# Moving one scratch tile to another ring, two gate additions to VectorE and two row scalings to ScalarE in a two-layer encoder

## The chip, the cores and the metric

The kernel runs on one core of one Trainium2 chip. A core has TensorE (matmul, with its weight load shown apart), VectorE, ScalarE, GpSimd and SyncE; the profile calls them PE and PEld, DVE, ACT, POOL and SP. They run their own instruction streams in order and wait for each other by semaphores. Operands lie in SBUF, matmul results in PSUM, inputs and outputs in device memory, and DMA engines move data between them. The metric is the device time of one execution in microseconds, as a median over several runs.

## The reference

Two layers on 512 tokens of width 1024, in float32. Layer 0 mixes tokens by neighbourhood attention on a grid, layer 1 by latent attention; then both add a gated embedding. A last norm follows.

```python
for i in range(DEPTH):
    xn = rmsnorm(x, norm_g[i])
    y = mixer_na(...) if i % 2 == 0 else mixer_mla(...)
    h = x + y
    gate = jax.nn.sigmoid(rmsnorm(h, ple_norm[i]) @ ple_w_gate[i])
    x = h + gate * (p[i] @ ple_w_proj[i])
return rmsnorm(x, final_norm)
```

where `rmsnorm(x, g)` is `x * rsqrt(mean(x * x) + 1e-6) * g`.

## The kernel before

The 512 tokens are four row tiles (0 to 3) of 128 partitions. [...] Precision comes from splitting every operand into a high and a low part, so that each product is three matmuls: high by high, low by high, high by low. `load_w` (lines 70 to 88) loads a weight tile as `wraw`, ScalarE makes the high part (line 83) and GpSimd the low part (line 84). Nearly all matmuls of projections are issued in the helper `mms` (line 107).

**Pools.** A tile comes from a pool; tiles of one tag share a ring of buffers and wait for the oldest to be free. `const`, `big`, `zp` and `wp` are opened first and stay: `big` holds transposed activations, `wp` the weights. `small` follows, for one-column tiles, with rings of eight for the tags `mx`, `sm`, `rc`, `ss`, `rs` and `mn` and one buffer for `warm`; each buffer takes 32 bytes of a partition. All pools opened later stand behind it: `pre` (start), `na` (heads of layer 0), `out0` and `out1` (output projection and gate of each layer), and `mla`, `mlac`, `mlah` (layer 1's heads). In `out0` and `out1` some of the weights lie in the stage's own pool instead of `wp`: those with `extra` in `load_w`, and in layer 1's gate those for which `own` in `prep` (line 577) is false.

**Heads.** In layer 1's dense heads the scores multiply `ke` or `ko` by `qe` or `qo`, `ex` holds the exponentials, four matmuls by `ident` transpose them (line 139), and line 841 multiplies them by the values. Projections of `cT` (line 730) stand between them.

**The last gate.** Layer 1's gate is `gate_seven`: a product of two matrices that are each cut in 2 x 2 blocks, made from seven block products instead of eight, in the order 1, 7, 2, 6, 5, 3, 4. Each product is two row tiles (i = 0, 1) of twelve matmuls at line 635, in two chunks of six; the weights of product p are prepared in two pieces by `prep(p)`, which loads, splits on ScalarE (line 587) and on GpSimd (line 589). The pieces of products 1 and 5 lie in `wp`, those of product 2 in `out1`, and product 3 has one of each. Products 2, 3, 5 and 4 each complete two pieces of the result, and `finish(t, n, ...)` is called for row tile t and column half n:

- ScalarE takes the sigmoid in PSUM (line 595);
- `pe`, the embedding, is loaded by DMA (line 600);
- VectorE multiplies (line 601), and the product is added to the row tile `r` (line 603), on VectorE if `last` is set and else on GpSimd;
- `after(t, n, ...)`, which is `done` of layer 1 (from line 1060 on), is kept in the list `behind` and traced when the next `finish` has traced its sigmoid.

`done` adds up the squares of the piece on ScalarE (line 1069, tile `sq`), or on VectorE for the very last quarter (line 1065), makes the mean `mn` on VectorE (line 1070), multiplies a tile's first half by the final norm's gain on GpSimd (line 1073), and once both halves of a row tile are there raises the mean to the power -1/2 on GpSimd (line 1079, `rs`), scales the half that came last by `rs` and gain on VectorE (line 1080), scales the first half by `rs` (on GpSimd, line 1082, for tiles 0 and 1; on ScalarE, line 1084, for tiles 2 and 3), and stores both.

The copies at line 647 take product 6 out of its bank, and product 5 adds onto it in that bank, so product 5 can start only behind the first of them.

**What sets the order.** The code is traced in program order with some edges (`issue_after`), and a scheduler orders each engine's stream from dependences and its own cost estimates; on the chip each engine then keeps that order. Tile numbers behind names, as in `r_6090`, are given by the build: `r_6090`, `r_6092`, `r_6094` and `r_6096` are row tiles 0 to 3.

Of the kernel before, what the change touches and what calls it, by code (L numbers as in the profile page):

```python
# [13 lines left out]
F32 = mybir.dt.float32  # L14
F32R = mybir.dt.float32r
AF = mybir.ActivationFunctionType
ALU = mybir.AluOpType
AX = mybir.AxisListType
PSUM = bass.MemoryType.PSUM
P = 128  # L20
S = 512
# [19 lines left out]
class Trunk:  # L41
# [527 lines left out]
    def gate_seven(self, pool, layer, rh, res, after):  # L569

        nc = self.nc
        pieces = 0
        turns = 3 + self.wxn // 2
        W, A, Bk, s1, s17, s6 = {}, {}, {}, {}, {}, {}

        def prep(p):
            nonlocal pieces
            W[p] = []
            src = self.quarter[layer][p] if p < 4 else self.sums[layer][p]
            for c in range(2):  # L580
                own = pieces % turns < 3
                pieces += 1
                raw = self.wp.tile([P, 1024], F32, name="wraw", tag="wraw", bufs=3)
                q, n = (self.wp, 3) if own else (pool, self.wxn)
                hi, lo = (q.tile([P, 1024], F32R, name=t, tag=t if own else "w4", bufs=n) for t in ("whi", "wlo"))
                nc.sync.dma_start(raw, src[c * P:(c + 1) * P])
                nc.scalar.activation(hi, raw, AF.Copy)  # L587
                for o in (slice(0, S), slice(S, 2 * S)):
                    nc.gpsimd.tensor_tensor(out=lo[:, o], in0=raw[:, o], in1=hi[:, o].bitcast(F32), op=ALU.subtract)  # L589
                W[p].append((hi, lo))  # L590

        behind = []

        def finish(t, n, x, o=0, wd=S, last=False):
            sg = nc.scalar.activation(x, x, AF.Sigmoid, scale=rh[t])
            while behind:
                with self.tc.issue_after(sg.ins):
                    behind.pop()()
            pe = pool.tile([P, S], F32, name="pe", tag="pe", bufs=4)[:, :wd]
            nc.sync.dma_start(pe, self.pe[layer][t][:, n * S + o:n * S + o + wd])  # L600
            nc.vector.tensor_tensor(out=x if last else pe, in0=pe, in1=x, op=ALU.mult)
            r = res[t][:, n * S + o:n * S + o + wd]
            (nc.vector if last else nc.gpsimd).tensor_tensor(out=r, in0=r, in1=x if last else pe, op=ALU.add)
            behind.append(lambda: after(t, n, o, wd))

        mm = self.last_out
        order = (1, 7, 2, 6, 5, 3, 4)
        for p in order[:4]:
            prep(p)
        warm = self.small.tile([P, 1], F32, name="warm", tag="warm", bufs=1)  # L610
        nc.scalar.activation(warm, rh[3], AF.Sigmoid)
        halves = ((0, 256), (256, 256)) if layer == 1 else ((0, S),)
        banks = {1: "mm", 7: "T", 6: "S"}
        home = {2: 1, 5: 6, 3: 6, 4: 7}
        C = {}
        sub = lambda out, x, y: nc.vector.tensor_tensor(out=out, in0=x, in1=y, op=ALU.subtract)
        for k, p in enumerate(order):
            if 0 < k < 4:
                prep(order[k + 3])
            if p == 7:  # L620
                self.mixed(5)
            if p == 6:
                self.mixed(3)
            x = self.X[p]
            for i in range(2):
                for o, wd in halves if i and p in (7, 4) else ((0, S),):
                    c = slice(o, o + wd)
                    if p in banks:
                        C[p, i, o] = self.psum("O" if o else banks[p])[:, :wd]
                    ps = C[home.get(p, p), i, o]  # L630
                    m = [(x[:, 2 * s + i, k * P:(k + 1) * P], W[p][k // 2][r][:, k % 2 * S + o:k % 2 * S + o + wd])
                         for c in range(2) for s, r in ((0, 0), (1, 0), (0, 1)) for k in (2 * c, 2 * c + 1)]
                    for j, (l, r) in enumerate(m):
                        with self.tc.issue_after(mm.ins):
                            mm = nc.tensor.matmul(ps, l, r, start=j == 0 and p in banks,  # L635
                                                  stop=j == 11 and p in (2, 3, 4), skip_group_check=True)
                    if p == 1:
                        s1[i] = self.temp("s1")
                        nc.scalar.activation(s1[i], ps, AF.Copy)
                    elif p == 7:  # L640
                        nc.vector.tensor_tensor(out=ps, in0=ps, in1=s1[i][:, c], op=ALU.add)
                        if o == 0:
                            s17[i] = self.temp("s17")
                        nc.scalar.activation(s17[i][:, c], ps, AF.Copy)
                    elif p == 6:
                        s6[i] = self.temp("s6")
                        nc.scalar.activation(s6[i], ps, AF.Copy)
                        for (a, b, o), t in C.items():
                            if (a, b) == (7, i):
                                sub(t, t, s6[i][:, o:o + t.shape[1]])  # L650
                    elif p == 5:
                        q = self.psum("mm" if i else "T")
                        sub(q, ps, s17[i])
                        sub(ps, ps, s1[i])
                        finish(2 + i, 1, q)
                    elif p == 2:
                        finish(i, 0, ps)
                    elif p == 3:
                        finish(i, 1, ps, last=layer == 1)
                    else:  # L660
                        finish(2 + i, 0, ps, o, wd, layer == 1)
        while behind:
            behind.pop()()

    def mla_c(self, pool, xT, cT, sets):
        nc, a = self.nc, self.a
# [273 lines left out]
    def run(self):  # L940
        tc, nc, a = self.tc, self.nc, self.a
# [6 lines left out]
        with tc.tile_pool(name="pre", bufs=4, reuse_waits="tile") as pool:  # L948
            ones = [nc.const_aps.tensor(1.0, (P, n), mybir.dt.bfloat16) for n in (P, S)]
            ps = self.psum("T")  # L950
# [26 lines left out]
            ss = pool.tile([P, NT], F32, name="ssq", bufs=1)  # L977
# [23 lines left out]
        with tc.tile_pool(name="na", bufs=2, reuse_waits="tile") as pool:  # L1001
            last = self.na_heads(pool, xT, zs, oT)

        x1T = []
        for layer in range(2):
            with tc.tile_pool(name=f"out{layer}", bufs=4, reuse_waits="tile") as pool:
                seven = layer in SEVEN
# [47 lines left out]
                else:  # L1055
                    mean = {}

                    def done(t, n, o, w):
                        c = slice(n * S + o, n * S + o + w)
                        r = res[t]  # L1060
                        sq = pool.tile([P, D], F32, name="sq", tag="xn", bufs=2 - seven)
                        mn = self.small.tile([P, 1], F32, name="mn", tag="mn")
                        first, final = t not in seen, o + w == S and t in seen
                        if o:
                            nc.vector.tensor_tensor_reduce(sq[:, :w], r[:, c], r[:, c], 1.0 / D, mean[t], op0=ALU.mult,
                                                           op1=ALU.add, accum_out=mn)
                        else:
                            ss = self.small.tile([P, 1], F32, name="ss", tag="ss")
                            nc.scalar.activation(sq[:, :w], r[:, c], AF.Square, accum_out=ss)
                            nc.vector.tensor_scalar(mn, ss, 1.0 / D, mean.get(t, EPS), op0=ALU.mult, op1=ALU.add)  # L1070
                        mean[t] = mn
                        if first:
                            nc.gpsimd.tensor_tensor(out=r[:, c], in0=r[:, c], in1=gn[:, c], op=ALU.mult)
                            seen.add(t)
                        if not final:
                            return
                        f, l = (slice(0, S), slice(S, D))[::1 if n else -1]
                        rs = self.small.tile([P, 1], F32, name="rs", tag="rs")
                        nc.gpsimd.tensor_tensor(out=rs, in0=mn, in1=self.half, op=ALU.pow)
                        nc.vector.scalar_tensor_tensor(r[:, l], r[:, l], rs, gn[:, l], op0=ALU.mult, op1=ALU.mult)  # L1080
                        if seven and n:
                            nc.gpsimd.tensor_tensor(out=r[:, f], in0=r[:, f], in1=rs.to_broadcast([P, S]), op=ALU.mult)
                        else:
                            nc.scalar.activation(r[:, f], r[:, f], AF.Copy, scale=rs)
                        nc.sync.dma_start(a["out"][t][:, l], r[:, l])
                        (nc.scalar if o else nc.sync).dma_start(a["out"][t][:, f], r[:, f])
                if seven:
# [115 lines left out]
```

## Time and profile before

| What | us |
|---|---|
| Median of 3 runs (lowest, highest) | 668.08 (667.8, 668.46) |
| The profiled execution | 668.41 |
| Its span, from the first to the last instruction | 666.3 |
| TensorE busy, of the span | 655.2 |
| GpSimd busy | 424.5 |
| ScalarE busy | 421.8 |
| VectorE busy | 372.0 |

The mean granted TensorE clock of the profiled execution is 0.995 of full speed. A row of the timeline gives the start and the length in us, the engine, the source line, the operation, the tiles written and read, and how many like instructions it merges; in square brackets stands the idle time before it and what ended that. A row of the chain of work gives start, length and what was being done; the chain is followed back from the last instruction, at each step to what released it. Rows of the groups give the busy time of all, then the mean of one in ns. A matmul's end is modelled in the profile, so the spacing of matmuls is read from their starts. The 9.2 us from 657.1 to the end hold 0.12 us of TensorE.

### The profile page before, as it was taken

Reading aid. Unit: us, or ns where it says so; the run is one execution under the profiler, and the core shown is the slowest. Engines: PE = TensorE matmul, PEld = TensorE weight load, DVE = VectorE, ACT = ScalarE, POOL = GpSimd, SP = SyncE. Lnnn points to the kernel's source line nnn. Section 1 sums busy time; section 2 is a strip of 40 time slices with the busy share of each in tenths; the row PEclk is TensorE's granted clock in tenths of the full one; section 3 lists DMA queues with packets and bytes.
Section 4 is the critical chain, followed back from the end, with each engine's and each line's share of the span. In section 5 each row is a group of like instructions: output and inputs, shape, how many; then the busy total and the mean of one; then the engine's idle time right before and its main releaser. Section 6 shows DMA issues by size and latency. Waiting matters only on the chain.

```text
span 666.3 us, 10037 instructions
## 1 busy us (share of the span) xinstructions
PE 655.2 (98%) x3443; PEld 555.2 (83%) x3443; DVE 372.0 (56%) x815; ACT 421.8 (63%) x838; POOL 424.5 (64%) x358
## 2 busy tenths in 40 slices
PE   9999999999999999999999999999999999999994
PEld 6888888988988888888899888888888888888873
DVE  6180365736645514443524613888888875144856
ACT  7671686857767742543444635887989887437944
POOL 0395466876575765853054526786959887748994
PEclk9999999999999999999999999999999999999998
DMA  9949422966142136534133335120111222664524
GB/s 323 343 149 329 159 89 90 206 154 162 58 146 76 64 141 253 190 103 139 79 111 108 106 94 154 53 76 18 54 49 63 65 89 103 229 244 160 166 93 150
DMA packets 37681, 90.62 MB, mean 136 GB/s; under 512 B 4416, under 2 KB 13376, under 8 KB 37568
## 3 DMA queue, kind: packets, MB, share of 16 engines
q1 hardware_dynamic: 33040, 85.02, 37.9%
q0 software_dynamic: 4160, 4.19, 4.0%
q10 hardware_dynamic: 432, 0.79, 0.3%
q8 instruction: 27, 0.44, 0.3%
q14 instruction: 22, 0.18, 0.1%
HBM read 78.45 MB, written 16.78 MB: 143 GB/s over the span
## 4 chain that ended last, share of the span: by engine, by line
PE 93%; POOL 2%; DMA 1%; issue 1%; DVE 1%; ACT 1%; POOLq 0%; DVEq 0%
PE ps_mm L107 42%; PE ps_S L107 13%; PE ps_mm L730 6%; PE ps_T L139 6%; PE ps_O L841 4%; PE ps_T L107 3%; PE ps_O L107 3%; PE ps_T L238 2%; PE ps_O L402 2%; PE ps_S L635 2%; PE ps_mm L184 2%; PE ps_T L390 2%; PE ps_mm L635 1%; PE ps_S L354 1%; PE ps_S L353 1%
## 5 line engine op out<-in xcount | busy, mean ns | idle before, releaser
L84 POOL TENSOR_TENSOR wwlo<-wraw,wwhi 128x1024 fp32r<-128x1024 f32 (+5 forms) x93 | 178.3, 1931 | 107.2 <-ACT wwhi L83 92.1
L83 ACT ACTIVATE wwhi<-wraw 128x1024 fp32r<-128x1024 f32 (+5 forms) x94 | 79.1, 863 | 74.6 <-issue 18.4
L826 POOL TENSOR_TENSOR ex<-ex,rc 128x512 f32<-128x512 f32 x64 | 66.3, 1048 | 25.4 <-DVE rc L825 18.1
L824 ACT ACTIVATE ex<-ps_S,mx 128x512 f32<-128x512 f32 x64 | 44.0, 687 | 12.2 <-DVE mx L822 11.1
L822 DVE TENSOR_REDUCE mx<-ps_S 128x1 f32<-128x512 f32 x64 | 43.7, 683 | 7.1 <-PE ps_S L107 6.5
L96 DVE TENSOR_TENSOR pt_lo<-ps_T,pt_hi 128x512 fp32r<-128x512 f32 x64 | 43.3, 682 | 7.7 <-ACT pt_hi L94 7.3
L376 POOL TENSOR_TENSOR ex<-ex,rc 128x128 f32<-128x128 f32 (+1 forms) x64 | 34.8, 583 | 18.1 <-DVE rc L372 18.1
L107 PE MATMUL ps_mm<-xh,wwhi 128*128 128x512 f32 x152 | 40.8, 399 | 0.0
L94 ACT ACTIVATE pt_hi<-ps_T 128x512 fp32r<-128x512 f32 x64 | 37.7, 595 | 4.5 <-PE ps_T L139 4.3
L139 PE MATMUL ps_T<-ident,ex 128*128 128x128 f32 x256 | 38.4, 272 | 0.0
L107 PE MATMUL ps_mm<-xl,wwhi 128*128 128x512 f32 x152 | 38.2, 391 | 0.0
L589 POOL TENSOR_TENSOR wlo<-wraw,whi 128x512 fp32r<-128x512 f32 x28 | 37.1, 1355 | 1.7 <-ACT whi L587 1.7
L107 PE MATMUL ps_mm<-xh,wwlo 128*128 128x512 f32 x152 | 38.1, 391 | 0.0
L139 PEld LDWEIGHTS ps_T<-ident,ex 128*128 128x128 f32 x256 | 31.5, 140 | 7.7 <-POOL ex L826 0.4
L107 PE MATMUL ps_mm<-wwhi,hnT 128*128 128x512 f32 x128 | 35.5, 397 | 0.0
L107 PEld LDWEIGHTS ps_mm<-xl,wwhi 128*128 128x128 f32 x152 | 28.4, 188 | 5.8
L205 DVE TENSOR_TENSOR u<-ps_O,u 64x512 f32<-64x512 f32 x32 | 22.0, 686 | 20.2 <-ACT u L204 19.6
L107 PEld LDWEIGHTS ps_mm<-xh,wwlo 128*128 128x128 f32 x152 | 28.3, 188 | 5.8
L370 ACT ACTIVATE ex<-ex,mx 128x128 f32<-128x128 f32 (+1 forms) x64 | 30.3, 475 | 1.8 <-DVE mx L360 0.8
L107 PEld LDWEIGHTS ps_mm<-xh,wwhi 128*128 128x128 f32 x152 | 27.3, 188 | 4.8
L107 PE MATMUL ps_S<-ke,qe 96*128 96x512 f32 x96 | 29.3, 411 | 0.1
L107 PE MATMUL ps_S<-ko,qo 128*128 128x512 f32 x96 | 28.9, 410 | 0.0
(435 smaller groups left out, 1775.6 us busy)
## 6 DMA issues: line engine op xcount, KB each, us to landing
wraw<-na_qk SPq DMA_DIRECT2D x16, 512.0 KB, 3.4
pe<-pe SPq DMA_DIRECT2D x31, 256.0 KB, 2.8
wraw<-gate SPq DMA_DIRECT2D x14, 512.0 KB, 3.3
wraw<-na_v SPq DMA_DIRECT2D x8, 512.0 KB, 3.4
wraw<-na_o SPq DMA_DIRECT2D x8, 512.0 KB, 3.4
wraw<-mla_z SPq DMA_DIRECT2D x8, 512.0 KB, 3.6
wraw<-mla_o SPq DMA_DIRECT2D x8, 512.0 KB, 3.5
wraw<-sum SPq DMA_DIRECT2D x8, 512.0 KB, 3.3
```

The costliest lines, as they stand in the source:

```text
L83: nc.scalar.activation(hi[:, c], raw[:, c], AF.Copy)
L84: f = lambda e, c=c: e.tensor_tensor(out=lo[:, c], in0=raw[:, c], in1=hi[:, c].bitcast(F32), op=ALU.subtract)
L94: self.last_copy = nc.scalar.activation(hi, src, AF.Copy, scale=scale)
L96: nc.vector.tensor_tensor(out=lo, in0=src, in1=hi.bitcast(F32), op=ALU.subtract)
L107: last = self.last_mm = nc.tensor.matmul(out, l, r, start=i == 0, stop=i == n - 1)
L139: self.last_mm = self.nc.tensor.transpose(t[:, i * P:(i + 1) * P], b, self.ident)
L376: self.last_norm = nc.gpsimd.tensor_tensor(out=e, in0=e, in1=rc[:, qt:qt + 1].to_broadcast([P, e.shape[1]]), op=ALU.mult)
L589: nc.gpsimd.tensor_tensor(out=lo[:, o], in0=raw[:, o], in1=hi[:, o].bitcast(F32), op=ALU.subtract)
L730: self.last_mm = nc.tensor.matmul(PS[key], *terms[i], start=i == 0, stop=i == len(terms) - 1)
L822: nc.vector.reduce_max(mx, sp, axis=AX.X, negate=True)
L824: nc.scalar.activation(ex, sp, AF.Exp, bias=mx, accum_out=sm)
L826: nc.gpsimd.tensor_tensor(out=ex, in0=ex, in1=rc.to_broadcast([P, S]), op=ALU.mult)
```

## The change

Four edits, none of which changes what is computed:

1. `warm`, a one-element tile that only brings in ScalarE's table for the sigmoid, takes a slot of the ring `ss` instead of a ring of its own. `small` then takes 32 bytes less per partition, and all pools opened after it start 32 bytes lower.
2. `finish` of product 2 (tiles 0 and 1, first half) sets `last`: VectorE's product stays in PSUM, and VectorE instead of GpSimd adds it to `r`.
3. `behind` is emptied from its front, and not while the first half of the split last piece (256 columns, `o` = 0) is finished, so tile 2's `done` is traced one sigmoid later.
4. The row scalings of tiles 0 and 1 that GpSimd made are made by ScalarE, as for tiles 2 and 3.

```diff
-        def finish(t, n, x, o=0, wd=S, last=False):
+        def finish(t, n, ps, o=0, wd=S, last=False):
+            x = ps
             sg = nc.scalar.activation(x, x, AF.Sigmoid, scale=rh[t])
-            while behind:
+            while behind and (o or wd == S):
                 with self.tc.issue_after(sg.ins):
-                    behind.pop()()
+                    behind.pop(0)()
             pe = pool.tile([P, S], F32, name="pe", tag="pe", bufs=4)[:, :wd]
             nc.sync.dma_start(pe, self.pe[layer][t][:, n * S + o:n * S + o + wd])
-            nc.vector.tensor_tensor(out=x if last else pe, in0=pe, in1=x, op=ALU.mult)
+            x = x if last else pe
+            nc.vector.tensor_tensor(out=x, in0=pe, in1=ps, op=ALU.mult)
             r = res[t][:, n * S + o:n * S + o + wd]
-            (nc.vector if last else nc.gpsimd).tensor_tensor(out=r, in0=r, in1=x if last else pe, op=ALU.add)
+            (nc.vector if last else nc.gpsimd).tensor_tensor(out=r, in0=r, in1=x, op=ALU.add)
...
-        warm = self.small.tile([P, 1], F32, name="warm", tag="warm", bufs=1)
+        warm = self.small.tile([P, 1], F32, name="warm", tag="ss")
...
-                        finish(i, 0, ps)
+                        finish(i, 0, ps, last=True)
...
-            behind.pop()()
+            behind.pop(0)()
...
-                        if seven and n:
-                            nc.gpsimd.tensor_tensor(out=r[:, f], in0=r[:, f], in1=rs.to_broadcast([P, S]), op=ALU.mult)
-                        else:
-                            nc.scalar.activation(r[:, f], r[:, f], AF.Copy, scale=rs)
+                        nc.scalar.activation(r[:, f], r[:, f], AF.Copy, scale=rs)
```

TensorE's and SyncE's streams keep their order. ScalarE's stream around the sigmoids of product 2 (`ps_mm`), the splits of the last two weight pieces (`whi`), tile 0's squares (`sq`) and the copies of product 6 (`s6`) is before

```order
L595 ACTIVATE ps_mm_6547<-ps_mm_6547,rs_6348 128x512
L587 ACTIVATE whi_6698<-wraw_6697 128x1024
L595 ACTIVATE ps_mm_6562<-ps_mm_6562,rs_6391 128x512
L587 ACTIVATE whi_6705<-wraw_6704 128x1024
L1069 ACTIVATE sq_6687,ss_6689<-r_6090 128x512
L647 ACTIVATE s6_6729<-ps_S_6716 128x512
L647 ACTIVATE s6_6745<-ps_S_6732 128x512
```

and with the change (line numbers of the changed file are one or two higher)

```order
L596 ACTIVATE ps_mm_6547<-ps_mm_6547,rs_6348 128x512
L587 ACTIVATE whi_6698<-wraw_6697 128x1024
L596 ACTIVATE ps_mm_6562<-ps_mm_6562,rs_6391 128x512
L1071 ACTIVATE sq_6687,ss_6689<-r_6090 128x512
L587 ACTIVATE whi_6705<-wraw_6704 128x1024
L649 ACTIVATE s6_6729<-ps_S_6716 128x512
L649 ACTIVATE s6_6745<-ps_S_6732 128x512
```

Tile 0's squares now stand ahead of the split of the last weight piece. At the program's end ScalarE's stream, with the last four sigmoids (`ps_S`, `ps_T`, `ps_O`), is before

```order
L595 ACTIVATE ps_S_6732<-ps_S_6732,rs_6391 128x512
L1069 ACTIVATE sq_6837,ss_6839<-r_6090 128x512
L595 ACTIVATE ps_T_6596<-ps_T_6596,rs_6439 128x512
L1069 ACTIVATE sq_6865,ss_6867<-r_6092 128x512
L595 ACTIVATE ps_T_6612<-ps_T_6612,rs_6485 128x256
L1069 ACTIVATE sq_6893,ss_6895<-r_6094 128x512
L595 ACTIVATE ps_O_6628<-ps_O_6628,rs_6485 128x256
L1069 ACTIVATE sq_6921,ss_6923<-r_6096 128x256
L1084 ACTIVATE r_6094<-r_6094,rs_6898 128x512
L1084 ACTIVATE r_6096<-r_6096,rs_6933 128x512
```

and with the change

```order
L596 ACTIVATE ps_S_6732<-ps_S_6732,rs_6391 128x512
L1071 ACTIVATE sq_6837,ss_6839<-r_6090 128x512
L1083 ACTIVATE r_6090<-r_6090,rs_6842 128x512
L596 ACTIVATE ps_T_6596<-ps_T_6596,rs_6439 128x512
L1071 ACTIVATE sq_6865,ss_6867<-r_6092 128x512
L596 ACTIVATE ps_T_6612<-ps_T_6612,rs_6485 128x256
L1083 ACTIVATE r_6092<-r_6092,rs_6870 128x512
L596 ACTIVATE ps_O_6628<-ps_O_6628,rs_6485 128x256
L1071 ACTIVATE sq_6910,ss_6912<-r_6094 128x512
L1071 ACTIVATE sq_6921,ss_6923<-r_6096 128x256
L1083 ACTIVATE r_6094<-r_6094,rs_6915 128x512
L1083 ACTIVATE r_6096<-r_6096,rs_6933 128x512
```

The scalings of tiles 0 and 1 stand each ahead of a sigmoid, and the squares of tile 2 moved behind the last sigmoid.

## The prediction

> **What bounds the kernel now.** The page comes first: the span, the busy time of TensorE, and the chain that ended last.
>
> ```profile
> span 666.3 us, 10037 instructions
> PE 655.2 (98%) x3443; PEld 555.2 (83%) x3443; DVE 372.0 (56%) x815; ACT 421.8 (63%) x838; POOL 424.5 (64%) x358
> PE 93%; POOL 2%; DMA 1%; issue 1%; DVE 1%; ACT 1%; POOLq 0%; DVEq 0%
> ```
>
> TensorE is busy almost throughout and holds 93% of the chain. Two things can therefore move the time: the spacing of matmuls, and the stretches in which the chain leaves TensorE. The chain in order of time shows two of those near the end, around 631 to 640 and from 651 on, both in code that the change touches.
>
> For the spacing I read the timeline of TensorE alone, in `gate_seven`. Each pair of rows below (4 and 2 matmuls) is one group of six with 512 columns; I take the start of one "x4" row from the next.
>
> ```profile
> 617.93 1.07 PE L635 MATMUL ps_mm<-whi,X 128*128 128x512 f32 x4
> ...
> 619.29 1.07 PE L635 MATMUL ps_mm<-whi,X 128*128 128x512 f32 x4
> ...
> 620.65 1.07 PE L635 MATMUL ps_mm<-whi,X 128*128 128x512 f32 x4
> ...
> 629.49 1.10 PE L635 MATMUL ps_mm<-whi,X 128*128 128x512 f32 x4
> ...
> 630.88 1.09 PE L635 MATMUL ps_mm<-whi,X 128*128 128x512 f32 x4
> ...
> 632.28 1.10 PE L635 MATMUL ps_mm<-whi,X 128*128 128x512 f32 x4
> ...
> 643.19 1.07 PE L635 MATMUL ps_S<-whi,X 128*128 128x512 f32 x4
> ...
> 644.55 1.07 PE L635 MATMUL ps_S<-whi,X 128*128 128x512 f32 x4
> ```
>
> Product 1 (617.93 to 620.65) takes 1.36 per six, product 2 (629.49 to 632.28) 1.395, product 5 (643.19 to 644.55) 1.36 again. Shapes, lines and the tile X are alike; what differs is where the other operand lies. The weights of products 1 and 5 lie in `self.wp`, those of product 2 in the stage's own pool (the `own` of `prep`). In the allocation of the built program `big` (X), `zp` and `wp` start 32 bytes past a multiple of 64, and every pool opened after `small` at a multiple of 64. So six matmuls lose 0.035 to 0.04 us, 6.7 ns each at the upper end, where the streamed operand and the weights of the next matmul stand in different halves of 64 bytes.
>
> **The change, part by part.**
>
> *Placement.* `small` keeps six tags of eight slots of 32 bytes and one slot for `warm`: 1568 bytes, 32 past a multiple of 64. Without that slot it is 1536, and all pools opened later move down by 32 bytes, which puts them where `big` and `wp` stand. Against this kernel they don't keep their place modulo 64; they take the one of the older pools. By the program's order and its addresses 775 matmuls of 512 columns have unlike halves now and like ones after: 299 before the dense heads (236 of them in the first output and gate stage), 265 in the heads, 51 from there to 594.3, 136 from 594.3 to 640.3, 24 later.
> - The 299 + 51 outside the heads: 350 x 6.7 ns = 2.35 us, on TensorE, which waits for nothing there.
> - The 265 in the heads: 1.78 us by the same price, but the timeline there is less clean:
>
> ```profile
> 471.14 0.87 PE L107 MATMUL ps_S<-ke,qe 96*128 96x512 f32 x3
> 471.85 0.86 PE L730 MATMUL ps_mm<-cT,wwhi 128*128 128x512 f32 x3
> 472.55 0.86 PE L730 MATMUL ps_mm<-cT,wwlo 128*128 128x512 f32 x3
> 473.25 0.60 PE L139 MATMUL ps_T<-ident,ex 128*128 128x128 f32 x4
> ```
>
>   ke and qe stand in like halves (one pool) and still take 0.71 for three, 237 ns; cT with wp, unlike, takes 1.40 for six, 233 ns. Something else costs time there too. Bounds 0 and 1.78; I take the middle, 0.89.
> - The 136 before 640.3: up to 0.91 us of TensorE, taken as 0, since the next piece shows that something else ends that stretch.
> - The 24 later: 0.16 us.
> - Narrower matmuls and the 492 transposes by `ident` (which stays at a multiple of 64 while their input moves away from it): no row shows such a transpose. The nearest are the 256-column matmuls, unlike first and like second:
>
> ```profile
> L107 PE MATMUL ps_mm<-wwhi,cT 128*128 128x256 f32 x48 | 7.7, 282 | 0.0
> L107 PE MATMUL ps_mm<-wwhi,xh 128*128 128x256 f32 x64 | 9.7, 287 | 0.0
> ```
>
>   282 against 287 ns shows no loss, so I take 0. The far bound is the loss of the wide ones in proportion, 0.04 of 1.36, so 3% of the 0.60 / 4 = 150 ns per transpose in the row at 473.25, 4.4 ns x 492 = 2.2 us; the other bound is a gain by the same 5 ns, 2.5 us, which I don't believe, as the two groups differ in stage.
>
> *The first two gate pieces (product 2).* The chain leaves TensorE here:
>
> ```profile
> 632.21 1.50 POOL wlo L589 x2
> ...
> 633.72 4.38 DMA wraw<-sum
> ...
> 638.13 1.06 ACT whi L587
> 639.19 0.30 ACT sq L1069
> ...
> 639.61 0.19 ACT sq L1069
> 639.80 0.49 ACT s L647
> ...
> 640.34 11.29 PE ps_S L635 x48
> ```
>
> ```profile
> 640.34 1.20 PE L635 MATMUL ps_S<-whi,X 128*128 128x512 f32 x4 [0.90 <-ACT s L647]
> ```
>
> TensorE waits 0.90 us for the copy of product 6 out of its bank. That copy stands in ScalarE's queue behind the split of the last weights, which waits for a DMA until 638.13, and behind `sq` (the sum of squares of tile 0), 0.61 us from 639.19 to 639.80. The change moves `sq` ahead of the split. It then waits for VectorE:
>
> ```profile
> 634.16 0.68 DVE L601 TENSOR_TENSOR pe<-pe,ps_mm 128x512 f32<-128x512 f32 x1
> 635.39 0.64 ACT L595 ACTIVATE ps_mm<-ps_mm,rs 128x512 f32<-128x512 f32 x1
> 650.29 0.69 DVE L603 TENSOR_TENSOR r<-r,ps_S 128x512 f32<-128x512 f32 x1
> ```
>
> The product ends at 634.84 and the addition, now on VectorE at the 0.69 of the third row, at 635.55; ScalarE is busy with the second sigmoid until 636.03. So `sq` runs from 636.0 to 636.7, inside the 2.1 us from 636.03 to 638.13 in which ScalarE has nothing but that DMA to wait for. Behind it queue the split, which GpSimd waits for, and both copies, which TensorE waits for; it delays them only if the addition ends after 637.5, 1.9 us late. The copy moves from 639.80 to 639.19, a gain of 0.61. TensorE comes 0.9 us earlier and waits longer: the next to end is the DMA chain. The two `pe` loads for product 3 go out earlier, as VectorE's product frees their buffers instead of GpSimd's later addition; in SP's queue they stay behind the weight load, but share the DMA engines with it. Bounds: 0 (that load as much later) and 1.8 (it lands early enough that nothing but TensorE's own 0.90 + 0.91 is left). GpSimd loses two additions and VectorE takes two of 0.69 between 634 and 638, where TensorE needs neither; taken at 0, covered by the same DMA wait.
>
> *The last row scalings and additions.* From 653 on the chain runs over VectorE:
>
> ```profile
> 653.86 1.63 DVE L1080 SCALAR_TENSOR_TENSOR r<-r,rs,gn 128x512 f32<-128x512 f32 x1
> 653.90 1.04 POOL L1082 TENSOR_TENSOR r<-r,rs 128x512 f32<-128x512 f32 x1
> ...
> 656.83 0.39 PE L635 MATMUL ps_O<-wlo,X 128*128 128x256 f32 x2
> 656.92 1.04 POOL L1082 TENSOR_TENSOR r<-r,rs 128x512 f32<-128x512 f32 x1
> ...
> 657.07 1.44 DVE L1080 SCALAR_TENSOR_TENSOR r<-r,rs,gn 128x512 f32<-128x512 f32 x1
> ...
> 657.54 0.43 ACT L595 ACTIVATE ps_O<-ps_O,rs 128x256 f32<-128x256 f32 x1
> 658.89 0.41 DVE L601 TENSOR_TENSOR ps_O<-pe,ps_O 128x256 f32<-128x256 f32 x1
> ...
> 659.63 0.72 ACT L1084 ACTIVATE r<-r,rs 128x512 f32<-128x512 f32 x1 [0.19 <-POOL rs L1079]
> ...
> 660.60 0.48 DVE L1065 CUSTOM_DVE_ANT_0 sq<-r,mn 128x256 f32<-128x256 f32 x1
> ...
> 661.17 0.55 POOL L1079 TENSOR_TENSOR rs<-mn,half 128x1 f32<-128x1 f32 x1 [1.57 <-DVE mn L1065]
> ...
> 661.75 0.75 DVE L1080 SCALAR_TENSOR_TENSOR r<-r,rs,gn 128x512 f32<-128x512 f32 x1 [0.66 <-POOL rs L1079]
> 662.50 0.38 ACTq L1086 DMA_DIRECT2D out<-r  x1
> ```
>
> VectorE's scaling takes 0.75 when GpSimd rests (last row but one) and 1.63 and 1.44 when GpSimd scales the other half of the same row. With both halves of tiles 0 and 1 off GpSimd, VectorE gets back 0.88 + 0.69 = 1.57 us. ScalarE takes two scalings of 0.72 instead. The first would run from 653.9 to 654.6 against a sigmoid that now starts at 654.46: 0.1 late. The second needs tile 1's `rs`, some 0.3 us earlier than now, and runs from about 656.6 to 657.3; the last sigmoid then goes from 657.3 to 657.75 (now 657.54 to 657.97), with the `sq` of tile 2 behind it. From there the last half tile on VectorE, with the rows' durations and about 0.05 between engines: product (0.41) to 658.2, tile 2's mean to 658.5, addition to 658.9, mean to 659.1, squares (0.48) to 659.6, the power on GpSimd (0.55) to 660.2, scaling (0.75) to 660.95. Now it ends at 662.50, so 1.55 less; I take 1.5. Bounds: 0.8, if the whole second scaling (0.72) falls before the last sigmoid, and 1.9, with the 0.3 us by which the mean of tile 1 comes early. The last store's 3.8 us behind 662.50 stay.
>
> *Sum.* The profiled execution took 668.41 us (span 666.3). 2.35 + 0.89 + 0 + 0.16 + 0.61 + 1.5 = 5.5 us less: 662.9. It stands 0.33 above the median of the runs, 668.08, so as a median 662.6.
>
> [...]
>
> **The rivals.**
> 1. *Placement does nothing.* What differs between products 1 and 2 is also the pool, not only its place modulo 64, and both move together in this trace. Against it: `big` and `wp` are two pools and run at 1.36. Only 0.61 + 1.5 remain: 666.0.
> 2. *TensorE's gain is taken back by GpSimd and ScalarE.* For it: GpSimd is busy 64% of the span, and the 631 to 640 chain shows how that looks. Then about a third of the placement terms arrives: 1.1 + 2.1, 664.9. Against it: 98% busy leaves little room for more such waits.
> 3. *Slower: the transposes.* If the unlike halves of `ident` and its input cost each of the 492 transposes 11 ns, they eat the 5.5 us; at twice that the kernel ends at 673.4. To be slower by a measurable 1.3 us it takes 14 ns on 150, three times the loss of the wide matmuls. Against it stand the two 256-column rows.
>
> **How the numbers follow.** The forecast has 0.72, with its own range 660.6 to 664.8 (heads in full and the DMA wait gone; heads and DMA term at 0 and 0.8 at the end). Rival 1 has 0.12, rival 2 0.09, rival 3 0.07. The whole range, 660.6 to 666.6, takes in rivals 1 and 2 with rival 1's middle term at 0, and leaves out rival 3. A measurement of this kernel can tell about 0.2%, 1.3 us, from no change. Faster by that: 0.72 + 0.09 + 0.08 of rival 1, 0.89 in all; within it 0.05 (the rest of rival 1 and a part of rival 3); slower 0.06.
>
> **What would show it.** Placement: six matmuls of product 2 in 1.36, and of `hnT` and `ww` likewise; groups of four transposes still at the 0.60 of the row at 473.25. Middle: `sq` of tile 0 before 637, TensorE's wait for the copy at 640 short of 0.9 or its start earlier relative to the weights' DMA. End: every VectorE scaling at 0.75, and 3.9 us instead of 5.3 from the last matmul's end to the last store's issue. The prediction is wrong if product 2 stays at 1.395, if transposes stretch, or if ScalarE's scalings hold up a sigmoid for longer than 0.2 us.

## The result, and the profile after

The changed kernel takes 664.51 us (median of four runs, 663.8 to 665.61) against 668.0 (four runs of the kernel before, 667.8 to 668.46): a ratio of 0.9948, 95% interval 0.9931 to 0.9965. A second set of runs, in the experiments below, gave 663.65 and 0.9934 (0.992 to 0.9947). The forecast was 662.6, its range 660.6 to 666.6: the side is right and the time lies in the range, but the gain is 3.5 to 4.1 us where 5.5 was expected.

The profiled execution took 664.19 us, 4.22 less than the one before. This is the head of its page and its summary of the chain:

```profile
span 662.4 us, 10036 instructions
...
PE 651.9 (98%) x3443; PEld 555.5 (84%) x3443; DVE 372.6 (56%) x817; ACT 422.9 (64%) x840; POOL 420.5 (63%) x354
...
PE 92%; POOL 3%; DMA 2%; issue 1%; ACT 1%; DVE 1%; POOLq 0%; ACTq 0%
```

TensorE still sets the time. Its matmuls are the same 3443 in the same order, so the two traces can be laid on each other start by start. TensorE is 1.36 us earlier at 400 us, 2.34 at 594, 2.81 at the first matmul of product 5 (637.53 instead of 640.34) and 2.93 at the last row of matmuls (653.90 instead of 656.83). From there to the issue of the last store it takes 4.74 us instead of 5.67. Together that is 3.86 of the span's 3.9.

The spacing first. The chain of work of the kernel before holds, in the first layer's gate, one unbroken piece of 143 matmuls,

```profile
288.56 33.14 PE ps_mm L107 x143
```

and so does that of the kernel after:

```profile
287.89 32.44 PE ps_mm L107 x143
```

231.7 ns per matmul became 226.9. The timeline of TensorE in the changed kernel shows product 2 of the last gate at the 1.36 per six that products 1 and 5 had before (626.69, 628.05, 629.41), and three rows from layer 1's heads:

```profile
470.06 0.86 PE L732 MATMUL ps_mm<-cT,wwhi 128*128 128x512 f32 x3
470.76 0.85 PE L732 MATMUL ps_mm<-cT,wwlo 128*128 128x512 f32 x3
471.45 0.60 PE L139 MATMUL ps_T<-ident,ex 128*128 128x128 f32 x4
...
626.69 1.07 PE L637 MATMUL ps_mm<-whi,X 128*128 128x512 f32 x4
...
628.05 1.07 PE L637 MATMUL ps_mm<-whi,X 128*128 128x512 f32 x4
...
629.41 1.07 PE L637 MATMUL ps_mm<-whi,X 128*128 128x512 f32 x4
```

In the heads nothing of the kind happened: two triples of `cT` still take 0.70 and 0.69, as before, although the halves are like now.

Ahead of product 5 the chain of the changed kernel reads

```profile
631.39 4.53 DMA wraw<-sum
...
637.53 11.19 PE ps_S L637 x48
```

and the timeline shows TensorE's wait, and the squares `sq` that moved ahead of the split:

```profile
633.61 0.62 ACT L1071 ACTIVATE sq<-r 128x512 f32<-128x512 f32 x1
...
635.94 1.06 ACT L587 ACTIVATE whi<-wraw 128x1024 fp32r<-128x1024 f32 x1 [1.61 <-DMA wraw<-sum]
636.90 1.06 ACT L649 ACTIVATE s<-ps_S 128x512 f32<-128x512 f32 x2
637.53 1.19 PE L637 MATMUL ps_S<-whi,X 128*128 128x512 f32 x4 [1.16 <-ACT s L649]
```

The squares are out of the way, and TensorE waits 1.16 us instead of 0.90 all the same: the copy still stands behind a split that waits for a DMA.

At the end, these rows of the timeline answer to the last ones of before:

```profile
653.77 0.72 ACT L1083 ACTIVATE r<-r,rs 128x512 f32<-128x512 f32 x1 [0.42 <-POOL rs L1081]
653.90 0.40 PE L637 MATMUL ps_O<-wlo,X 128*128 128x256 f32 x2
653.95 0.74 DVE L1082 SCALAR_TENSOR_TENSOR r<-r,rs,gn 128x512 f32<-128x512 f32 x1
654.40 0.43 ACT L596 ACTIVATE ps_O<-ps_O,rs 128x256 f32<-128x256 f32 x1
...
656.70 0.75 DVE L1082 SCALAR_TENSOR_TENSOR r<-r,rs,gn 128x512 f32<-128x512 f32 x1
656.86 0.99 POOL L1081 TENSOR_TENSOR rs<-mn,half 128x1 f32<-128x1 f32 x1 [0.52 <-DVE mn L1067]
...
657.89 0.75 DVE L1082 SCALAR_TENSOR_TENSOR r<-r,rs,gn 128x512 f32<-128x512 f32 x1 [0.44 <-POOL rs L1081]
658.64 0.38 ACTq L1085 DMA_DIRECT2D out<-r  x1
```

VectorE's scalings take 0.75 each, where two of them took 1.63 and 1.44. But the last power on GpSimd, one column, now takes 0.99 where it took 0.55, and it runs beside VectorE's scaling of tile 2.

### The profile page after: what moved, and what is told of

It is laid out like the page before. It is cut to its first block, busy times and chain, and to the rows that moved or that the text cites. A ratio compares the mean times of both kernels' runs of the same rounds, so it can differ in the third digit from the quotient of the medians.

```text
span 662.4 us, 10036 instructions
## 1 busy us (share of the span) xinstructions
PE 651.9 (98%) x3443; PEld 555.5 (84%) x3443; DVE 372.6 (56%) x817; ACT 422.9 (64%) x840; POOL 420.5 (63%) x354
## 4 chain that ended last, share of the span: by engine, by line
PE 92%; POOL 3%; DMA 2%; issue 1%; ACT 1%; DVE 1%; POOLq 0%; ACTq 0%
PE ps_mm L107 42%; PE ps_S L107 13%; PE ps_mm L732 6%; PE ps_T L139 6%; PE ps_O L843 4%; PE ps_T L107 3%; PE ps_O L107 3%; PE ps_T L238 2%; PE ps_O L402 2%; PE ps_S L637 2%; PE ps_mm L184 2%; PE ps_T L390 2%; POOL wlo L589 1%; PE ps_S L354 1%; PE ps_S L353 1%
```

## The experiments

Each kernel below ran beside the kernel before on the same chip; times are medians, ratios are to the kernel before with their 95% interval.

### The placement alone, and everything but the placement

`e_place` is the kernel before with one edit; every engine's order stays.

```diff
-        warm = self.small.tile([P, 1], F32, name="warm", tag="warm", bufs=1)
+        warm = self.small.tile([P, 1], F32, name="warm", tag="ss")
```

> The kernel before with one edit: `warm` takes a slot of the tag `ss`. The order of every engine stays that of before, and the pools opened after `small` stand 32 bytes lower, in the same half of 64 bytes as `big`, `zp` and `wp`. Theory (like halves are quicker): the shift of TensorE's starts seen in the changed kernel up to 594 us, 2.25, and 0.16 at the end: 2.4 us less than 668.0, so 665.6; six matmuls of product 2 in 1.36 instead of 1.395; nothing gained around 640 and nothing in the tail. Rival (placement does nothing, the order of the additions shifted TensorE): 668.0, product 2 at 1.395.

665.68 us against 667.84, ratio 0.9973 (0.9962 to 0.9983). `e_rest` is the changed kernel with that line put back.

> The changed kernel with `warm` in its own ring again: all other edits, without the move of the pools. Theory: only the middle (0.55) and the tail (0.95) stay, 1.5 less than 668.0: 666.5; product 2 at 1.395 again, VectorE's scalings at 0.75, the last power at 0.99. Rival (placement does nothing): 664.5 as the changed kernel.

665.8 us against 667.84, ratio 0.997 (0.9958 to 0.9981). The chain of `e_place` has the piece of 143 matmuls at the changed kernel's length,

```profile
287.86 32.44 PE ps_mm L107 x143
```

and that of `e_rest` at the length of before:

```profile
288.50 33.14 PE ps_mm L107 x143
```

Product 2's groups of six take 1.36 in `e_place` and 1.40 in `e_rest`, as expected. The granted clock doesn't explain this: the profiled execution of `e_place` has 0.995, like that of the kernel before, and that of `e_rest` 0.998, like that of the changed kernel. So the quicker spacing comes with the placement and with nothing else, and it is 2.2 of the gain. The two parts by themselves gave 2.16 and 2.04, 4.2 together, where the whole change gave 3.5 and 4.1 in its two sets of runs. In `e_place` TensorE is 2.40 us earlier at 594 and 3.14 at the last matmul; product 5 starts 3.02 earlier, so the expectation that nothing is gained there was wrong in this trace. Its chain shows by what:

```profile
613.89 2.52 PE ps_mm L635 x11
616.41 3.45 POOL wlo L589 x3
...
631.32 3.77 DMA wraw<-sum
...
635.11 1.06 ACT whi L587
...
637.32 11.19 PE ps_S L635 x48
```

The chain now leaves TensorE at 616.41, for GpSimd's splits, where before it stayed on TensorE until 631.06: what TensorE gains behind that point is swallowed. The last load can start 2.40 us earlier (631.32 instead of 633.72), which is 0.42 less than TensorE's lead at 616 (2.82). The other 0.61 is the load itself, which took 3.77 us there and 4.38 in the trace of before.

`e_rest` gained half a microsecond more than expected. Its timeline says where:

```profile
635.94 0.62 ACT L1071 ACTIVATE sq<-r 128x512 f32<-128x512 f32 x1
637.33 1.06 ACT L587 ACTIVATE whi<-wraw 128x1024 fp32r<-128x1024 f32 x1 [0.67 <-DMA wraw<-sum]
```

The split starts at 637.33, 0.8 us sooner than the 638.13 of the kernel before, since the same load took 3.6 us. The wait is gone altogether, and product 5 starts 1.12 us earlier. This load takes a different time in each trace (3.6, 3.77, 4.38, 4.53), even in two traces of one kernel: the changed kernel's 4.53 is 3.72 in `after_again`, below. What the moved squares are worth is therefore read from its landing on: to product 5's start it takes 2.24 us in the kernel before (638.10 to 640.34) and 2.23 in `e_place` (635.09 to 637.32), where the squares stand behind the split, and 1.61 in the changed kernel (635.92 to 637.53). That is 0.63. Other traces agree: 2.23 in `e_far64` and `e_scale`, and 1.62 in `e_zero`, `e_psum` and `after_again`.

### Is it the half of 64 bytes?

`e_far64` is the kernel before with all later pools moved, but by a whole 64 bytes; `e_zero` is the changed kernel with `big`, `zp`, `wp` and all later pools at a multiple of 64 instead of 32 past it.

```diff
-        warm = self.small.tile([P, 1], F32, name="warm", tag="warm", bufs=1)
+        warm = self.small.tile([P, 1], F32, name="warm", tag="warm", bufs=3)
```

> The kernel before with three slots for `warm` instead of one: the later pools move up by 64 bytes and keep their half of 64 bytes, unlike that of `big`, `zp` and `wp`. Theory: 668.0, within 0.3; product 2 at 1.395. Rival (any other distance between the tiles would do, the half of 64 bytes has nothing to do with it): a change as large as the placement's, 666.0 or less.

```diff
+        nc.vector.memset(self.const.tile([P, 1], F32, name="pad"), 0.0)
```

> The changed kernel with a 32-byte tile `pad` in the pool `const`, which is never read: `big`, `zp`, `wp` and all later pools stand at a multiple of 64, and `ident` with them. Theory (being in like halves matters, not the value 32): 664.5, within 0.4; product 2 at 1.36. Rival 1 (a start 32 past a multiple of 64 is what is quick): about 667, every group of 512 columns back at 1.395 for six. Rival 2 (transposes by `ident` against unlike halves cost up to 5 ns each in the changed kernel): up to 2.4 less, 662.

`e_far64`: 668.02 against 667.84, ratio 1.0007 (0.9998 to 1.0015). `e_zero`: 664.06, ratio 0.9948 (0.9935 to 0.996). The chain of `e_far64` has

```profile
288.50 33.22 PE ps_mm L107 x143
```

and the groups of the first layer's gate, whose figures behind the first bar are the busy time and the mean of one in ns, read in the kernel before

```profile
L107 PE MATMUL ps_mm<-wwhi,hnT 128*128 128x512 f32 x128 | 35.5, 397 | 0.0
L107 PE MATMUL ps_mm<-wwlo,hnT 128*128 128x512 f32 x64 | 20.1, 395 | 0.0
```

and in `e_zero`

```profile
L108 PE MATMUL ps_mm<-wwhi,hnT 128*128 128x512 f32 x128 | 34.9, 392 | 0.0
L108 PE MATMUL ps_mm<-wwlo,hnT 128*128 128x512 f32 x64 | 19.8, 392 | 0.0
```

Product 2's groups take 1.40 in `e_far64` and 1.36 in `e_zero`. Moving the pools alone gains nothing (at 639 us TensorE is 0.16 later in `e_far64` than before), and neither does the value 32: what counts is whether the two operands stand in like halves of 64 bytes. A quick placement moved by 64 bytes was not run, so these placements don't tell halves of 64 from like places in a larger block, such as 128. `ident` and its inputs are in like halves again in `e_zero`, and it is no quicker than the changed kernel by more than the two sets of runs of that differ (664.51, 663.65). Start by start, within groups, the changed kernel's transposes take 108.7 ns as they did before.

### The end: the scalings alone, and the last power

`e_scale` is the kernel before with the fourth edit only.

```diff
-                        if seven and n:
-                            nc.gpsimd.tensor_tensor(out=r[:, f], in0=r[:, f], in1=rs.to_broadcast([P, S]), op=ALU.mult)
-                        else:
-                            nc.scalar.activation(r[:, f], r[:, f], AF.Copy, scale=rs)
+                        nc.scalar.activation(r[:, f], r[:, f], AF.Copy, scale=rs)
```

> The kernel before with one edit: the row scalings of the last stage all on ScalarE, none on GpSimd. Theory (VectorE's scaling was held up by GpSimd's on the same row): VectorE's scalings at 0.75 instead of 1.63 and 1.44, the stretch from the last matmul's start to the end shorter by 0.9 to 1.0, so 667.1; the last power on GpSimd takes 0.99 here as well, since VectorE's scaling of tile 2 runs beside it. Rival (the tail's gain came with the additions' order or with the earlier matmuls): 668.0, or the last power at 0.55 and 1.4 less, 666.6.

667.07 against 667.88, ratio 0.9988 (0.9979 to 0.9997). Its timeline at the end:

```profile
656.52 0.39 PE L635 MATMUL ps_O<-wlo,X 128*128 128x256 f32 x2
...
657.01 0.61 ACT L1069 ACTIVATE sq<-r 128x512 f32<-128x512 f32 x1
...
657.62 0.43 ACT L595 ACTIVATE ps_O<-ps_O,rs 128x256 f32<-128x256 f32 x1
...
660.32 0.55 POOL L1079 TENSOR_TENSOR rs<-mn,half 128x1 f32<-128x1 f32 x1 [1.73 <-DVE mn L1065]
...
661.65 0.38 ACTq L1083 DMA_DIRECT2D out<-r  x1
```

The time is the expected one, but in part by luck: in the trace TensorE ends 0.31 us earlier because the last load took only 3.66 us, and the end gains less than expected. VectorE's scalings take 0.75 here too, but from the last row of matmuls to the last store's issue it takes 5.13 us: 0.54 less than before, not 0.9 to 1.0. The last sigmoid waits behind tile 2's squares until 657.62. The other 0.4 (4.74 in the changed kernel, and 4.72 in `e_rest`) goes to the third edit, by which those squares come behind the last sigmoid; it was not run alone, and the order of the rows is the evidence for it. And the power takes 0.55 here, not 0.99 as expected, because VectorE's scaling of tile 2 is over by then. By the same argument it is the third edit that brings the two together.

`e_psum` is the changed kernel with tile 2's last sum left in PSUM, for the squares and the scaling to read.

```diff
+            if (t, n) == (2, 0):
+                self.kept = x
+            out = x if (t, n) == (2, 0) else r
-            (nc.vector if last else nc.gpsimd).tensor_tensor(out=r, in0=r, in1=x, op=ALU.add)
+            (nc.vector if last else nc.gpsimd).tensor_tensor(out=out, in0=r, in1=x, op=ALU.add)
...
-                        nc.vector.scalar_tensor_tensor(r[:, l], r[:, l], rs, gn[:, l], op0=ALU.mult, op1=ALU.mult)
+                        nc.vector.scalar_tensor_tensor(r[:, l], piece if t == 2 else r[:, l], rs, gn[:, l], op0=ALU.mult, op1=ALU.mult)
```

> The changed kernel; the last addition of tile 2's first half leaves its sum in PSUM, and the sum of squares and the scaling read it there, so that VectorE's scaling beside the last power has one operand in SBUF instead of two. Theory (the power took 0.99 instead of 0.55 because of that scaling): the last power at 0.55, 0.4 less, 664.1. Rival (the power is slow there for another reason): 0.99 again, 664.5.

663.49 against 667.88, ratio 0.9934 (0.9921 to 0.9947). Its timeline:

```profile
653.64 0.40 PE L640 MATMUL ps_O<-wlo,X 128*128 128x256 f32 x2
...
656.41 0.75 DVE L1086 SCALAR_TENSOR_TENSOR r<-ps_T,rs,gn 128x512 f32<-128x512 f32 x1
656.58 0.55 POOL L1085 TENSOR_TENSOR rs<-mn,half 128x1 f32<-128x1 f32 x1 [0.52 <-DVE mn L1071]
...
657.91 0.38 ACTq L1089 DMA_DIRECT2D out<-r  x1
```

The power overlaps VectorE's scaling as in the changed kernel and takes 0.55: only the scaling's first operand is elsewhere. So the power's extra 0.44 us came from this scaling's two operands in SBUF. From the last matmuls to the last store's issue it takes 4.27, 0.47 less than in the changed kernel. The trace is the evidence for this: the changed kernel's own two medians (664.51 and 663.65) lie further apart than 0.47. Which of the two engines is held up is not settled by the starts. In the changed kernel's trace the power came second (656.86, the scaling 656.70) and ended 0.40 after the scaling. In the second pair of before GpSimd's scaling came first (656.92), and VectorE's, of 1.44, ended 0.55 after it. In the first pair VectorE's row, of 1.63, begins 0.04 ahead of GpSimd's (653.86 and 653.90), and yet VectorE is the one held up, again until 0.55 after GpSimd's end.

### The copy behind the split

`e_split_late` is the changed kernel with the split of the last weight piece behind the copies of product 6 in ScalarE's queue; the other engines' orders stay.

```diff
-            if 0 < k < 4:
+            if 0 < k < 3:
                 prep(order[k + 3])
...
-                nc.scalar.activation(hi, raw, AF.Copy)
+                with self.tc.issue_after(self.copied.ins) if p == 4 and c else nullcontext():
+                    nc.scalar.activation(hi, raw, AF.Copy)
...
-                        nc.scalar.activation(s6[i], ps, AF.Copy)
+                        self.copied = nc.scalar.activation(s6[i], ps, AF.Copy)
...
                     elif p == 5:
+                        if i == 0:
+                            prep(4)
```

> The changed kernel; the split of the last weight piece of product 4 stands in ScalarE's queue behind the two copies of product 6 out of its bank, instead of ahead of them. No other engine's order changes. Theory (the copies were late only because they queue behind a split that waits for a DMA): TensorE's wait of 1.16 at 637.5 is gone, and the last matmul starts 1.1 earlier: 663.4. Rival 1 (the copies, or the next product, wait for something else that ends at the same time: a free tile, weights): 664.5. Rival 2 (the split, later by 2 us, and GpSimd's subtractions behind it hold up product 4): slower than 664.5, with a wait of TensorE ahead of ps_T at 648.

663.23 against 667.88, ratio 0.9933 (0.992 to 0.9946). The timeline of ScalarE and TensorE:

```profile
634.80 0.58 ACT L650 ACTIVATE s<-ps_S 128x512 f32<-128x512 f32 x1
...
635.20 1.07 PE L638 MATMUL ps_S<-whi,X 128*128 128x512 f32 x4
...
636.56 1.07 PE L638 MATMUL ps_S<-whi,X 128*128 128x512 f32 x4
...
636.82 0.60 ACT L650 ACTIVATE s<-ps_S 128x512 f32<-128x512 f32 x1 [1.44 <-PE ps_S L638]
637.32 1.05 ACT L588 ACTIVATE whi<-wraw 128x1024 fp32r<-128x1024 f32 x1
```

Product 5 follows product 6 (the row at 636.56 after that at 635.20) at the usual 1.36, with no wait, and the last matmuls start 1.11 us earlier than in the changed kernel's trace (652.79 and 653.90). The split, 1.4 us later, holds up nothing. In this trace the copies were late only because of what stood ahead of them.

### Both, and the changed kernel once more

`e_best` and `best_again` are the changed kernel with the edits of `e_split_late` and `e_psum`; `after_again` is the changed kernel as it is, beside `best_again`.

> The changed kernel with both edits, the later split of product 4's last weights and tile 2's sum kept in PSUM. Theory: the two gains lie on the same chain one after the other and add up, 1.1 + 0.4 less than 664.5: 663.0. Rival: one of them is swallowed by the other's neighbour, 663.4 or 664.1.

> The changed kernel as it is, beside the next on one chip. Theory (its copies of product 6 stand behind a split that waits for a DMA whose landing differs from execution to execution: 635.92 in its trace, 635.11 with the placement alone): 664.0 to 664.8, its own executions spread over more than 1 us. Rival (its first four executions were off by chance): under 663.6, or a spread under 0.5.

> The changed kernel with the later split and tile 2's sum in PSUM, beside the changed kernel on one chip. Theory: 662.8, a spread under 0.8, since no copy that TensorE waits for is behind a DMA any more, and 1.3 to 1.9 less than the changed kernel. Rival (the gain lay in the chip or the day): less than 0.8 below the changed kernel.

`e_best`: 662.84 against 667.88, ratio 0.9924 (0.991 to 0.9938). `after_again`: 663.65 (663.35 to 664.55) against 667.8, ratio 0.9934. `best_again`: 662.91 (662.48 to 663.53), ratio 0.9925 (0.9912 to 0.9937). The two edits beat both kernels: their ten executions took 662.48 to 663.53, the changed kernel's nine 663.35 to 665.61. But side by side they are 0.74 apart, not 1.3 to 1.9. That is under the 0.8 which the rival had named, so this pair of runs doesn't exclude that a part of the larger gain was the chip or the day; `after_again` itself came out below its 664.0 to 664.8. And the spread of `best_again`, 1.05, is above the 0.8 that was expected, so the DMA ahead of the copy isn't the only source of the spread. The profiled execution of `after_again` shows another one, in the heads:

```profile
412.23 0.50 PE L107 MATMUL ps_S<-ke,qe 96*128 96x512 f32 x1 [0.71 <-DMA qe<-rl]
```

The trace of the changed kernel has no such wait there; that of `e_scale` has one of 0.44. How often it strikes, and whether an earlier TensorE makes it likelier, wasn't measured.

The same trace shows one reason why the later split can bring less than 1.1 us. TensorE's wait ahead of product 5 is short in it:

```profile
637.89 1.19 PE L637 MATMUL ps_S<-whi,X 128*128 128x512 f32 x4 [0.35 <-ACT s L649]
```

Among the kernels with the squares ahead of the split this wait is 1.16 in the changed kernel's first trace, 0.87 in `e_psum`, 0.35 here, 0.22 in `e_zero` and 0 in `e_rest`. It is what the later split can remove, so its gain differs from execution to execution, and the 1.1 of the first trace is the largest that a trace shows.

## Why the prediction was right or wrong

| Term | Predicted | Measured |
|---|---|---|
| Placement, outside the heads, and in the heads | 2.35 + 0.89 | 2.34 up to 594 us |
| Up to the start of product 5 (136 unlike matmuls at 0, the squares at 0.61) | 0.61 | 0.47 |
| After product 5's start | 0.16 | 0.12 |
| The end | 1.5 | 0.93 |
| Sum, of the span | 5.5 | 3.86 |

**Placement: the effect was right, its price too high and not valid everywhere.** It was shown by taking it alone, by undoing it alone, and by the two other placements. Whether it is the weights of the next matmul that count, as the prediction has it, or a matmul's own was not shown. The step that failed is the choice of 6.7 ns, the upper end of 1.395 to 1.40 against 1.36; the lower end is 5.8 ns. The 236 unlike matmuls of the first output and gate stage gained 1.36 us and the 51 between the heads and 594 us 0.30, 5.8 ns each. The `cT` matmuls just ahead of the dense heads also gained at this price (234 to 227 ns). The second part that failed is the step that took narrower matmuls at 0. In the first layer's heads the lead fell from 0.18 at 100 us to 0.03 at 242: the matmuls of 512 columns gained 0.1 there, and those of 256 columns lost 0.2 (several groups went from 118 to 120 ns). `e_far64`, which keeps the halves, loses 0.13 on them, and `e_rest`, which moves nothing, 0.0; so this loss comes with the move and not with the half, and its cause is open. In the dense heads (413 to 570 us) TensorE gained 0.46, about half of the 0.89 that was taken, and not for the reason behind it. The projections of `cT`, which stood in unlike halves before, gained 0.12 on 132 matmuls, 0.9 ns each; the scores of `ke` and `qe`, in like halves before and after, gained 0.29 on 94, and they gain as much in `e_far64`. What costs time in the heads, where matmuls of 512 columns stay at 231 to 235 ns, was not settled.

**The 136 at 0 and the squares at 0.61: right.** Product 5 starts 2.81 us earlier: the last load starts 2.33 earlier (631.39 instead of 633.72), the squares bring 0.63 behind its landing, and the load itself took 0.15 longer. That the DMA chain ends the stretch was right, and that TensorE's own gain is lost in it; TensorE's wait grew from 0.90 to 1.16. What the prediction did not see is that the chain leaves TensorE 15 us sooner than before, and that one load's time differs by up to 1.0 us between traces (3.55 in `e_far64`, 4.53 in the changed kernel), more than the term. The two `pe` loads beside it were one possible cause; in `e_rest` they went out as soon behind the load's start (1.1 us), and it took 3.6.

**The end: two parts right, one missing.** The scalings at 0.75 came as forecast, and ScalarE's scalings held up a sigmoid by about 0.1, not by the 0.2 that would have spoken against it. From the last matmul's end to the last store's issue 3.9 us were forecast and 4.34 measured. What failed is the step "the power on GpSimd (0.55)": it took 0.99. The prediction had such a loss for VectorE's scalings (1.63 and 1.44 against 0.75), but did not ask for one in GpSimd's power, which the third edit puts beside one of them. With that removed, in `e_psum`, the stretch is 3.87.

**The transposes at 0** were right. **The range.** By its own terms the low end of the forecast's own range comes to 660.5 and not 660.6, which changes nothing here. **The rivals.** Placement does nothing: refuted by `e_place`, where it alone takes 143 matmuls from 33.14 us to 32.44. Gain taken back by GpSimd and ScalarE: it happened in part, from 616 us to product 5, but of the placement terms of 3.4 us two thirds arrived (2.2), not one. Slower by the transposes: refuted.

## What to carry to other kernels

Before pricing a move of pools, list for each group of matmuls in which half of 64 bytes its streamed operand and its weights stand; like halves were worth 5.8 ns of 233 per matmul of 512 columns in this kernel's output and gate stages, at no cost in instructions, and much less in layer 1's heads. A copy that TensorE waits for should not stand in a queue behind work that waits for a DMA: asking what is ahead of it found a wait of up to 1.16 us that the change had left. Taking it out, together with the last power's 0.4, was worth 0.74 us of the median time side by side. And when work is moved off an engine pair that hinder each other, go through all remaining pairs that now overlap, the one-column ones too: here the power, 0.99 us instead of 0.55.

## What the runs showed of the hardware

In the four placements that ran, a matmul of 512 columns (float32, split) is spaced at 227 ns in the output and gate stages when the operand that it streams and the weights stand in like halves of 64 bytes, be it both at 0 or both at 32, and at about 233 otherwise (product 2: 1.36 for six in `e_place` and `e_zero`, 1.40 in `before` and `e_far64`). In layer 1's heads it stayed at 231 to 235. Transposes showed no difference (108.7 ns before and after). A power on a single column of GpSimd grew from 0.55 to 0.99 us beside a VectorE instruction with two SBUF operands, and not beside the same one with an operand in PSUM (`after`, `e_psum`). A VectorE scaling of 128 x 512 with two SBUF operands took 0.75, and 1.63 and 1.44 beside GpSimd's scaling of the other half of the row (`before`). A weight load of 512 KB took 3.55 to 4.53 us in traces of kernels that issue it at the same place of its queue (`e_far64`, `after`).
